# A 31-tap convolution on VectorE, its second channel tile's taps dealt out between the blocks of an attention

## The chip, the cores and the metric

The kernel runs on one core of a Trainium2 chip. The metric is the device time of one execution in microseconds (us). Of the runs of a kernel the median is given.

## What is computed

Two layers, each of a mixer and a feed-forward part, on 512 positions of 1024 features in float32. The mixer splits one projection into four branches and projects their concatenation back:

```python
za, zq, zkv, zg, zc, zd = jnp.split(rms_norm(x, g) @ w_in[l], offsets, axis=-1)
y_conv = conformer_conv(za, ...)      # gate, 31-tap causal depthwise conv, layer_norm, silu
y_nsa  = nsa_attention(q, kv, ...)    # compressed + selected + window attention, 4 heads of 64
y_sgu  = spatial_gating(zc, ...)      # gelu, layer_norm of v, 128x128 causal mix, times u
y_pool = multiscale_pool(zd, ...)     # running means over 2, 4, 8, 16
x = x + rms_norm(jnp.concatenate([y_conv, y_nsa, y_sgu, y_pool], -1) @ w_out[l], g2)
x = x + rms_norm(conv_ffn(rms_norm(x, g3), ...), g4)
```

Attention works on four blocks of 128 queries. With 512 positions all key blocks are selected, so block `i` has scores of width 128 (i + 1) in each of two branches (selected, window), and a third branch over 31 compressed keys.

## The kernel before

Activations lie with features on partitions, 128 to a tile. A product in float32 precision is three matmuls of a split into high and low parts (`product`, lines 149, 152 and 153); `split` makes the two parts of an activation, `yh`/`yl`, on ScalarE and VectorE or GpSimd.

`mixer` runs named steps in the order of the table `STEPS`. Their instructions are then put into one queue for each engine by a scheduler that models the times of the engines; each engine works its queue in order. So the table, data and buffers set the order together. `behind` adds an order between two instructions without a wait of its own.

The steps that matter here, by name:
- `taps`: 26 of the 31 taps of the depthwise convolution, for two channel tiles `j`, on VectorE (line 681, the first tap line 679), each adding to a PSUM accumulator `acc[j]` of pool tag `c`. Tile 1 runs `AHEAD = 12` taps behind tile 0, and the two alternate. `others` makes the last five taps on ScalarE and GpSimd, `sum` adds them.
- `cn` (`conv_norm`): the layer norm of the convolution and its Silu. A matmul with ones gives the mean (line 709), VectorE subtracts it, ScalarE squares, a second matmul with ones gives the variance (line 239 in `stats`), ScalarE takes the root, VectorE the reciprocal (line 242), GpSimd multiplies, ScalarE makes the Silu (line 722) and `split` the tiles y[0] and y[1].
- `a0` to `a3` and `b0` to `b3` (`scores`): for a block and a branch, four heads' scores on TensorE (lines 782 to 786), the maxima on VectorE (line 788), the exponentials on ScalarE (line 790), then the scaling of the probabilities (line 796).
- `p0` to `p3` (`values`): transposes of the probabilities (line 807), their copies out of PSUM (lines 811 on VectorE, 813 on ScalarE), the products with the values (line 816), at the end the compressed branch's (line 819), into y[2] and y[3].
- `cmp2` and `probs`: the compressed branch; its probabilities are multiplied on GpSimd and transposed by TensorE (line 752).
- `v`, `w`, `su`, `fg`: spatial gating, with the normalisation of v on VectorE; `fg` (line 658) makes y[4] and y[5].
- `pool0`, `pool1`, `fp`: pooling; `fp` (line 608) makes y[6] and y[7].

Behind the mixer comes `out_proj`, with y in the order 4, 5, 6, 7, 0, 1, 2, 3. Products whose y is there already can be placed by the scheduler among the last attention blocks.

PSUM has eight banks, handed out by pool tag: `s` 2, `t` 1, `o` 1, `mm` 2, `c` 2. Scores use `s`, and for blocks 2 and 3 `c` as a third bank; transposes `t`, and for blocks 2 and 3 also `c`.

Of the kernel before, what the change touches and what calls it, by code (L numbers as in the profile page):

```python
# [10 lines left out]
OP = mybir.AluOpType  # L11
AX = mybir.AxisListType

L, D, S = 2, 1024, 512
# [4 lines left out]
TAPS = 31  # L19
# [37 lines left out]
class Kernel:  # L57
# [6 lines left out]
    P_DVE, PT_DVE = ((2, 3), (2,), (0, 1), ()), (1, 0, 0)  # L64

    SQ_POOL = (1,), (1, 2, 3, 4, 5, 6, 7)

    AHEAD = 12

    LAST_POOL = (1, 4)  # L70

# [318 lines left out]
    def first_weights(self, l):  # L390
        return [self.weights(l, u) for u in (U_KK, U_CMP, U_Q, U_Q + 1)]

    STEPS = ("conv0", "consts", "conv1", "cmp", "kk", "q1", "nat", "w", "q0", "gates", "a1", "cmp2", "taps", "probs", "su",
             "v", "pool0", "a0", "b0", "b1", "p0", "p1", "pool1", "a2", "b2", "p2", "a3", "fp", "b3", "p3", "fg",
             "others", "sum", "cn")

    def mixer(self, l):
        nc = self.nc
# [5 lines left out]
        n = 512 if l == 0 else 256  # L404
# [4 lines left out]
        gl = [self.slot(f"z{j}", F, (128, 544)) for j in range(2)]  # L409
        acc = [None, None]  # L410
# [3 lines left out]
        def proj(u, tag="mm"):  # L414
            ps = self.ps(tag)
            m["proj"] = self.product(ps, self.weights(l, u), range(KT), h)
            return ps
# [88 lines left out]
        def probs():  # L506
# [4 lines left out]
        steps = {  # L511
            "consts": constants, "nat": nat, "gates": gates, "kk": keys, "cmp": lambda: m.update(g1=self.compressed(l, psc)),
            "cmp2": lambda: self.compressed_out(m["g1"]), "probs": probs,
            "su": lambda: self.gating_u([proj(U_SU + j) for j in range(2)]),
            "v": lambda: self.gating_v(m["nat"]), "w": self.gating_w, "fg": lambda: self.gating_finish(m["nat"]),
            "taps": lambda: self.taps(gl, acc), "others": lambda: self.other_taps(gl),
            "sum": lambda: self.taps_sum(acc), "fp": self.pool_finish, "cn": lambda: self.conv_norm(acc)}
# [4 lines left out]
        for i in range(4):  # L522
# [2 lines left out]
                    {(i, b): self.scores(i, b, m["gates"], Q2, KH, KL)})  # L525
            steps[f"p{i}"] = lambda i=i: self.values(i, [m[i, b] for b in range(2)], m["nat"], m["pcT"])
        for name in self.STEPS:
            steps[name]()

    def compressed(self, l, ps):  # L530

# [136 lines left out]
    def taps(self, gl, acc):  # L668

        nc = self.nc  # L670
        acc[:] = [self.ps("c") for _ in range(2)]
        n = TAPS - self.OTHER_TAPS
        for i in range(n + self.AHEAD):
            for j, k in ((0, i), (1, i - self.AHEAD)):
                if not 0 <= k < n:
                    continue
                x, w = gl[j][:, k:k + S], self.col("taps", j * TAPS + k)
                if k == 0:
                    nc.vector.tensor_scalar(acc[j], x, w, self.col("conv_b", j), op0=OP.mult, op1=OP.add)
                else:  # L680
                    nc.vector.scalar_tensor_tensor(acc[j], x, w, acc[j], op0=OP.mult, op1=OP.add)  # L681

    def other_taps(self, gl):
        nc = self.nc
# [73 lines left out]
    def scores(self, i, b, gates, Q2, KH, KL):  # L758

        nc = self.nc
        w = (i + 1) * 128
        e = max(w, 256)
        per = 1 if i > 1 else 2
        if i == 0:
            p = self.slot(("yh6", "yl6")[b])
            P = [p[:, 128 * s:128 * s + 128] for s in range(4)]  # L770
        elif i == 1:
            p = [self.slot("yh7"), self.slot("yl7")] if b == 0 else [self.tmp(), self.tmp()]
            P = [p[s // 2][:, 256 * (s % 2):256 * (s % 2) + 256] for s in range(4)]
        else:
            P = [self.slot(f"hl{4 * b + s}")[:, :w] for s in range(4)]
        sm = self.mp.tile([128, 3, 4], F, name="sm", tag="sm", bufs=3)
        for s0 in range(0, 4, per):
            ps = self.ps(("s", "s", "c")[self.sc % 3] if i > 1 else "s")
            self.sc += 1
            for s in range(s0, s0 + per):  # L780
                q, o = Q2[ORDER[s]][:, i * 128:(i + 1) * 128], 256 * (s - s0)
                nc.tensor.matmul(ps[:, o:o + e], q, KH[b][:, :e], start=s == s0, stop=False, skip_group_check=True)
                self.scored = nc.tensor.matmul(ps[:, o:o + e], q, KL[b][:, :e], start=False, stop=False,
                                               skip_group_check=True)
            src = ps.rearrange("p (s k) -> p s k", s=per)[:, :, :w]
            nc.tensor.matmul(src[:, :, w - 128:], self.identb, self.maskb[:, None, :].to_broadcast([128, per, 128]),
                             start=False, stop=True, skip_group_check=True)
            nc.vector.tensor_reduce(sm[:, 0, s0:s0 + per], src, axis=AX.X, op=OP.max, negate=True)
            for s in range(s0, s0 + per):
                nc.scalar.activation(P[s], src[:, s - s0], AF.Exp, bias=sm[:, 0, s:s + 1],  # L790
                                     accum_out=sm[:, 1, s:s + 1])
        nc.vector.reciprocal(sm[:, 2], sm[:, 1])
        self.tt(sm[:, 2], sm[:, 2], gates[:, 1 + b, 4 * i:4 * i + 4], OP.mult)
        for s in range(4):
            eng = nc.vector if s in self.P_DVE[i] else nc.gpsimd
            eng.tensor_scalar(P[s], P[s], sm[:, 2, s:s + 1], 0.0, op0=OP.mult, op1=OP.add)
        return P

    def values(self, i, P2, nat, pcT):

        nc = self.nc
        O = self.ps("o")
        for b, P in enumerate(P2):
            for kb in range(i + 1):
                pst = self.ps(("t", "c")[self.pt % 2] if i > 1 else "t")
                for s in range(4):
                    nc.tensor.transpose(pst[:, s * 128:(s + 1) * 128], P[s][:, kb * 128:(kb + 1) * 128], self.ident)
                PT = self.tmp() if i < 2 else self.slot(f"hh{self.pt % 8}")
                self.pt += 1
                if self.PT_DVE[self.pt % len(self.PT_DVE)]:  # L810
                    nc.vector.tensor_copy(PT, pst)
                else:
                    nc.scalar.activation(PT, pst, AF.Copy)
                v = nat[:, kb, 256 + 64 * b:320 + 64 * b]
                for c in range(2):
                    nc.tensor.matmul(O[64 * c:64 * c + 64, :256], v, PT[:, 256 * c:256 * c + 256],  # L816
                                     start=b == 0 and kb == 0, stop=False, skip_group_check=True)
        for t in range(2):
            nc.tensor.matmul(O[:, t * 128:(t + 1) * 128], self.vcbd[:, t * 128:(t + 1) * 128],
                             pcT[:, i * 128:(i + 1) * 128], start=False, stop=t == 1, skip_group_check=True)  # L820
        for t in range(2):
            c = slice(i * 128, (i + 1) * 128)
            hi, lo = self.y[2 + t]
            nc.scalar.activation(hi[:, c], O[:, t * 128:(t + 1) * 128], AF.Copy)
            self.tt(lo[:, c], O[:, t * 128:(t + 1) * 128], hi[:, c].bitcast(F), OP.subtract)
# [117 lines left out]
def layouts(i):  # L943
# [30 lines left out]
    for n, ph in enumerate(PHASES):  # L974
        for j in range(8):
# [10 lines left out]
    out["vec"] = np.concatenate(  # L986
        [part(i[n]) for n in ("norm_mix_pre", "norm_mix_post", "norm_ffn_pre", "norm_ffn_post", "conv_dw_b",
                              "conv_ln_g", "conv_ln_b", "pool_scale", "sgu_ln_g", "sgu_ln_b")] + [pe, taps, fw, fb], axis=2)
    out["sgu_b"] = i["sgu_b"]
    out["wst"] = i["sgu_w"].transpose(0, 3, 1, 2)  # L990
# [52 lines left out]
```

## Time and profile before

| | |
|---|---|
| three runs | 1198.51, 1198.56, 1205.59 us; median 1198.56 |
| the profiled execution | 1195.33 us, span 1193.5 us |
| TensorE busy | 1132.3 us, 95% |
| VectorE busy | 746.2 us, 63% |
| ScalarE busy | 597.6 us, 50% |
| GpSimd busy | 553.9 us, 46% |

The span is the stretch that the trace covers; the execution's own time is 1.8 us longer. The shares are averages over the whole span. The mixers take up about 40 to 175 us (layer 0) and 640 to 765 us (layer 1); the rest is output projection, norms and feed-forward.

### The profile page before, as it was taken

What the parts mean: (1) busy time and instruction counts of PE and PEld (TensorE: products, weight loads), DVE (VectorE), ACT (ScalarE), POOL (GpSimd) and SP (SyncE); (2) the same over time, 40 slices, a digit from 0 to 9 for tenths busy, and PEclk for the clock granted to TensorE, in tenths of its full rate; (3) what the DMA queues carried; (4) which work ended last, traced back from release to release, by engine and by line L of the source; (5) the groups of instructions that cost most, each with busy time, mean ns of one, the idle gap of its engine ahead of it and who ended that gap; (6) DMA issues with size and microseconds to landing.
All of it is one profiled execution on the core that took longest, in us unless ns stands there. A gap on an engine that the chain in (4) does not pass through costs nothing.

```text
span 1193.5 us, 15945 instructions
## 1 busy us (share of the span) xinstructions
PE 1132.3 (95%) x6070; PEld 938.4 (79%) x6070; DVE 746.2 (63%) x1076; ACT 597.6 (50%) x973; POOL 553.9 (46%) x480
## 2 busy tenths in 40 slices
PE   7998999898999999999989979999999999999995
PEld 6786579886888888888978856899868888888894
DVE  5799734786076614774568997247942665157736
ACT  7777656554334323333657956564543443233431
POOL 1354443365655555554244544424656555455532
PEclk9999899999999999999999989999999999999997
DMA  8869015423432323223638660162233332322302
GB/s 266 225 161 215 12 49 145 103 85 93 141 90 96 97 96 99 89 89 88 165 63 212 148 158 1 35 166 64 95 102 124 93 102 71 123 89 89 90 35 71
DMA packets 43213, 129.35 MB, mean 108 GB/s; under 512 B 6144, under 2 KB 9856, under 8 KB 43136
## 3 DMA queue, kind: packets, MB, share of 16 engines
q1 hardware_dynamic: 35648, 102.01, 27.1%
q0 software_dynamic: 7488, 26.32, 11.9%
q8 instruction: 48, 0.79, 0.3%
q14 instruction: 29, 0.24, 0.1%
HBM read 126.21 MB, written 2.10 MB: 108 GB/s over the span
## 4 chain that ended last, share of the span: by engine, by line
PE 64%; DVE 19%; DMA 7%; ACT 6%; issue 3%; SPq 1%; POOL 0%; DVEq 0%; ACTq 0%
PE ps_s L153 7%; PE ps_s L149 7%; PE ps_s L152 7%; PE ps_mm L149 7%; PE ps_mm L153 7%; PE ps_mm L152 6%; PE ps_c L149 6%; PE ps_c L152 6%; PE ps_c L153 6%; DMA raw<-in_ws_dram 5%; DVE ps_c L681 4%; DVE q L888 2%; PE ps_o L816 2%; DVE yl L101 2%; DVE q L101 1%
## 5 line engine op out<-in xcount | busy, mean ns | idle before, releaser
L101 POOL TENSOR_TENSOR wlo<-raw,whi 128x512 fp32r<-128x512 f32 (+1 forms) x252 | 358.1, 1445 | 304.5 <-ACT whi L126 290.3
L126 ACT ACTIVATE whi<-raw 128x1024 fp32r<-128x1024 f32 (+2 forms) x180 | 183.7, 1024 | 156.8 <-DMA raw<-in_ws_dram 59.1
L149 PE MATMUL ps_mm<-hh,whi 128*128 128x512 f32 (+1 forms) x368 | 141.4, 384 | 9.6 <-ACT nat L447 3.9
L153 PE MATMUL ps_mm<-hh,wlo 128*128 128x512 f32 (+1 forms) x368 | 140.4, 382 | 1.8 <-DMA wlo<-in_ws_dram 1.7
L888 DVE SCALAR_TENSOR_TENSOR q<-q,vec,q 128x511 f32<-128x511 f32 (+1 forms) x88 | 115.4, 1317 | 40.4 <-ACT q L885 39.1
L152 PE MATMUL ps_mm<-hl,whi 128*128 128x512 f32 (+1 forms) x368 | 139.8, 380 | 0.0
L135 POOL DMA_DIRECT2D wlo<-in_ws_dram x52 | 45.9, 886 | 171.8 <-ACT wlo L134 118.5
L149 PE MATMUL ps_s<-hh,whi 128*128 128x512 f32 (+1 forms) x312 | 115.7, 373 | 8.5 <-ACT whi L362 7.1
L152 PE MATMUL ps_s<-hl,whi 128*128 128x512 f32 (+1 forms) x312 | 116.4, 373 | 1.2 <-DVE hl L278 1.1
L153 PE MATMUL ps_s<-hh,wlo 128*128 128x512 f32 (+1 forms) x312 | 115.1, 369 | 2.2 <-DMA wlo<-in_ws_dram 2.2
L153 PE MATMUL ps_c<-hh,wlo 128*128 128x512 f32 (+1 forms) x288 | 107.1, 372 | 1.5 <-DMA wlo<-in_ws_dram 1.5
L149 PE MATMUL ps_c<-hh,whi 128*128 128x512 f32 (+1 forms) x288 | 107.4, 373 | 0.8 <-ACT hh L273 0.8
L152 PE MATMUL ps_c<-hl,whi 128*128 128x512 f32 (+1 forms) x288 | 107.0, 372 | 0.0
L149 PEld LDWEIGHTS ps_mm<-hh,whi 128*128 128x128 f32 x368 | 70.5, 191 | 24.8 <-ACT nat L447 4.1
L153 PEld LDWEIGHTS ps_mm<-hh,wlo 128*128 128x128 f32 x368 | 70.4, 191 | 16.6 <-DMA wlo<-in_ws_dram 2.3
L149 PE MATMUL ps_mm<-yh,whi 128*128 128x256 f32 (+1 forms) x236 | 79.4, 336 | 2.8 <-ACT yh L158 2.7
L152 PEld LDWEIGHTS ps_mm<-hl,whi 128*128 128x128 f32 x368 | 70.6, 192 | 13.8
L152 PE MATMUL ps_mm<-yl,whi 128*128 128x256 f32 (+1 forms) x236 | 78.5, 333 | 0.2 <-DVE yl L101 0.2
L153 PE MATMUL ps_mm<-yh,wlo 128*128 128x256 f32 (+1 forms) x236 | 78.6, 333 | 0.0
L888 DVE SCALAR_TENSOR_TENSOR kl<-kl,vec,kl 128x511 f32<-128x511 f32 (+1 forms) x44 | 58.8, 1336 | 25.9 <-ACT kl L885 25.2
L149 PEld LDWEIGHTS ps_s<-hh,whi 128*128 128x128 f32 x312 | 59.1, 189 | 20.0 <-ACT whi L362 7.1
L152 PE MATMUL ps_s<-yl,whi 128*128 128x512 f32 (+1 forms) x222 | 73.6, 332 | 0.0
(331 smaller groups left out, 2670.7 us busy)
## 6 DMA issues: line engine op xcount, KB each, us to landing
raw<-in_ws_dram SPq DMA_DIRECT2D x156, 512.0 KB, 3.6
wlo<-in_ws_dram POOLq DMA_DIRECT2D x44, 512.0 KB, 7.3
raw<-in_ws_dram SPq DMA_DIRECT2D x16, 384.0 KB, 3.1
tmp<-in_w_dram SPq DMA_DIRECT2D x16, 256.0 KB, 5.3
raw<-in_ws_dram SPq DMA_DIRECT2D x8, 396.0 KB, 4.1
wlo<-in_ws_dram POOLq DMA_DIRECT2D x8, 396.0 KB, 7.4
x<-in_xt_dram SPq DMA_DIRECT2D x8, 256.0 KB, 5.4
out_dram<-x SPq DMA_DIRECT2D x16, 128.0 KB, 1.8
```

What stands on the lines that cost most here:

```text
L101: return (eng or self.nc.vector).tensor_tensor(out, x, y, op=op)
L126: one = nc.scalar.activation(hi[:, :cols], raw[:, :cols], AF.Copy)
L135: nc.gpsimd.dma_start(lo[:, :cols], src, accum_op=OP.add)
L149: one = nc.tensor.matmul(ps, wh, ah, start=start and n == 0, stop=False)
L152: nc.tensor.matmul(ps, wh, al, start=False, stop=False)
L153: one = nc.tensor.matmul(ps, wl, ah, start=False, stop=stop and n == len(ks) - 1)
L681: nc.vector.scalar_tensor_tensor(acc[j], x, w, acc[j], op0=OP.mult, op1=OP.add)
L816: nc.tensor.matmul(O[64 * c:64 * c + 64, :256], v, PT[:, 256 * c:256 * c + 256], start=b == 0 and kb == 0, stop=False, skip_group_check=True)
L888: nc.vector.scalar_tensor_tensor(t[:, s:], v[:, :S - s], fw(k), t[:, s:], op0=OP.mult, op1=OP.add)
```

## The change

The taps of tile 0 now run alone, ahead of `a1`. Tile 1's 26 taps are cut into groups (`"t0:5"` is taps 0 to 4), and each tap of a group is put behind the maxima that were written last, `self.topped`. The compressed branch (`cmp2`, `probs`), `su` and `a0` now come ahead of `v` and the pooling steps, `p0` ahead of `pool1`, `fg` ahead of `b2` and `fp` behind `p2`. The third bank of blocks 2 and 3 comes from tag `mm` in place of `c`, for scores and for transposes. No operation is added or left out.

```diff
-    AHEAD = 12
...
-    STEPS = ("conv0", "consts", "conv1", "cmp", "kk", "q1", "nat", "w", "q0", "gates", "a1", "cmp2", "taps", "probs", "su",
-             "v", "pool0", "a0", "b0", "b1", "p0", "p1", "pool1", "a2", "b2", "p2", "a3", "fp", "b3", "p3", "fg",
-             "others", "sum", "cn")
+    STEPS = ("conv0", "consts", "conv1", "cmp", "kk", "q1", "nat", "w", "q0", "gates", "taps", "a1", "t0:0",
+             "cmp2", "probs", "su", "a0", "t0:5", "v", "b0", "t5:10", "b1", "t10:14", "pool0", "p0", "pool1",
+             "p1", "a2", "t14:18", "fg", "b2", "t18:22", "p2", "fp", "a3", "t22:26", "b3", "p3", "others",
+             "sum", "cn")
...
         for name in self.STEPS:
-            steps[name]()
+            if ":" in name:
+
+                self.some_taps(gl, acc, 1, range(*map(int, name[1:].split(":"))), self.topped)
+            else:
+                steps[name]()
...
         acc[:] = [self.ps("c") for _ in range(2)]
-        n = TAPS - self.OTHER_TAPS
-        for i in range(n + self.AHEAD):
-            for j, k in ((0, i), (1, i - self.AHEAD)):
...
+        self.some_taps(gl, acc, 0, range(TAPS - self.OTHER_TAPS))
+
+    def some_taps(self, gl, acc, j, ks, behind=None):
+        nc = self.nc
+        for k in ks:
+            x, w = gl[j][:, k:k + S], self.col("taps", j * TAPS + k)
+            if k == 0:
+                one = nc.vector.tensor_scalar(acc[j], x, w, self.col("conv_b", j), op0=OP.mult, op1=OP.add)
+            else:
+                one = nc.vector.scalar_tensor_tensor(acc[j], x, w, acc[j], op0=OP.mult, op1=OP.add)
+            self.behind(one, behind)
...
-            ps = self.ps(("s", "s", "c")[self.sc % 3] if i > 1 else "s")
+            ps = self.ps(("s", "s", "mm")[self.sc % 3] if i > 1 else "s")
...
-            nc.vector.tensor_reduce(sm[:, 0, s0:s0 + per], src, axis=AX.X, op=OP.max, negate=True)
+            self.topped = nc.vector.tensor_reduce(sm[:, 0, s0:s0 + per], src, axis=AX.X, op=OP.max, negate=True)
...
-                pst = self.ps(("t", "c")[self.pt % 2] if i > 1 else "t")
+                pst = self.ps(("t", "mm")[self.pt % 2] if i > 1 else "t")
```

Line numbers of the changed kernel differ by -2 to +4: maxima stand in line 792, taps in 684 (the first of a tile in 682), transposes in 811, the values' products in 820 and 823, the ones matmuls of `conv_norm` in 713 and 237.

VectorE's queue in layer 1 before, around block 0's maxima of the second branch (line 788, the first such row here; `z_5427` and `z_5428` are the padded inputs of the convolution's tiles 0 and 1, `z_6664` the sum of tile 0, the `cmx` rows the compressed branch):

```order
L681 SCALAR_TENSOR_TENSOR ps_c<-z_5427,vec,ps_c 128x512
L101 TENSOR_TENSOR sm<-sm,gates 128x4
L101 TENSOR_TENSOR z_6291<-ps_mm,rsx 128x512
L101 TENSOR_TENSOR z_6099<-yh_6102,z_6099 64x16
L788 TENSOR_REDUCE sm<-ps_s 128x2 x2
L681 SCALAR_TENSOR_TENSOR ps_c<-z_5428,vec,ps_c 128x512
L101 TENSOR_TENSOR cmx<-cmx,gates 128x16
L101 TENSOR_TENSOR z_6099<-yl_6104,z_6099 64x16
L101 TENSOR_TENSOR z_6664<-ps_c,yh_6636 128x512
```

The same engine in the changed kernel, from the sum of tile 0 to the first taps of tile 1; the maxima here are those of block 0's first branch:

```order
L99 TENSOR_TENSOR z_6664<-ps_c,yh_6636 128x512
L636 TENSOR_SCALAR nat<-nat,bmv,bsd 128x256 x4
L99 TENSOR_TENSOR z_6018<-ps_mm,rsx 128x512
L745 TENSOR_REDUCE cmx<-ps_o 128x16
L792 TENSOR_REDUCE sm<-ps_s 128x2 x2
L682 TENSOR_SCALAR ps_c<-z_5428,vec 128x512
L99 TENSOR_TENSOR tmp<-ps_o,cmx 128x512
L684 SCALAR_TENSOR_TENSOR ps_c<-z_5428,vec,ps_c 128x512
L796 RECIPROCAL sm<-sm 128x4
```

Before, tile 0 is finished and tile 1 nearly so when block 0's second maxima are taken; now tile 0 is finished ahead of the first, and tile 1 begins behind them.

TensorE's queue in layer 1 before, at the variance matmul of `conv_norm` (line 239; `hl` are probabilities of block 3, `yh_6616` a tile of y[4] to y[7] in a product of the output projection, `whi` and `wlo` its weights):

```order
L807 MATMUL ps_t<-ident,hl_6491 128x128
L807 MATMUL ps_c<-ident,hl_6491 128x128 x2
L239 MATMUL ps_mm<-tmp,ones 128x512
L807 MATMUL ps_t<-ident,hl_6492 128x128
L807 MATMUL ps_c<-ident,hl_6492 128x128 x2
L149 MATMUL ps_mm<-yh_6616,whi 128x256
L152 MATMUL ps_mm<-yl_6617,whi 128x256
L153 MATMUL ps_mm<-yh_6616,wlo 128x256
```

The same engine in the changed kernel, at the variance matmul (line 237):

```order
L811 MATMUL ps_t<-ident,hl_6525 128x128
L820 MATMUL ps_o<-hh_6617,nat 64x256 x2
L820 MATMUL ps_o<-hh_6626,nat 64x256 x2
L823 MATMUL ps_o<-pct,vcbd 128x128 x2
L237 MATMUL ps_mm<-tmp,ones 128x512
L147 MATMUL ps_mm<-yh_6347,whi 128x256
L150 MATMUL ps_mm<-yl_6348,whi 128x256
L151 MATMUL ps_mm<-yh_6347,wlo 128x256
```

The variance matmul has moved from among block 3's transposes to behind the last matmul of p3 (line 823). Behind it stand 24 matmuls of 256 columns, then the first product with a normalised tile, `yh_6684`; in layer 0 12 of 512 and 12 of 256 columns.

## Rows read from the trace of the kernel before

**Rows 1.** The page: busy times; the chain by engine; loads on SP's queue.

```profile
PE 1132.3 (95%) x6070; PEld 938.4 (79%) x6070; DVE 746.2 (63%) x1076; ACT 597.6 (50%) x973; POOL 553.9 (46%) x480
...
PE 64%; DVE 19%; DMA 7%; ACT 6%; issue 3%; SPq 1%; POOL 0%; DVEq 0%; ACTq 0%
...
raw<-in_ws_dram SPq DMA_DIRECT2D x156, 512.0 KB, 3.6
```

**Rows 2.** Windows: length, busy time of PE, PEld, DVE, ACT, POOL; then granted clock.

```profile
110.00:120.00 10.00, 5.82 (x32) 4.42 (x31) 7.99 (x21) 4.80 (x15) 7.34 (x8) 0.81 0.92 201
120.00:130.00 10.00, 8.84 (x44) 5.61 (x42) 8.77 (x24) 6.78 (x23) 5.90 (x9) 0.68 0.04 7
690.00:700.00 10.00, 8.95 (x45) 6.86 (x44) 10.00 (x19) 7.03 (x14) 3.19 (x4) 1.00 1.06 261
700.00:710.00 10.00, 3.56 (x14) 2.88 (x15) 9.84 (x25) 3.11 (x15) 6.75 (x8) 0.67 0.49 112
710.00:720.00 10.00, 9.26 (x53) 6.32 (x53) 9.73 (x27) 6.60 (x21) 4.32 (x8) 0.82 0.01 2
```

**Rows 3.** The same view of the two stretches at the lower clock.

```profile
116.00:126.00 10.00, 8.06 (x30) 5.28 (x31) 7.25 (x22) 6.02 (x24) 6.27 (x9) 0.51 0.38 72
703.30:713.20 9.90, 6.76 (x26) 5.16 (x27) 9.80 (x26) 5.03 (x20) 7.39 (x9) 0.50 0.28 55
```

**Rows 4.** TensorE's waits over the span: total, times, longest.

```profile
PE ps_s L782 <- ACT yl L790: 6.6, 2, 5.8
...
PE ps_t L752 <- POOL tmp L101: 2.7, 1, 2.7
```

**Rows 5.** The chain that ended last, in layer 1: start, length, what.

```profile
665.58 8.10 DVE ps_c L681 x13
...
703.88 0.67 DVE sm L788 x2
```

**Rows 6.** Timeline of VectorE at the end of layer 1's mixer.

```profile
752.90 3.35 DVE L242 RECIPROCAL tmp<-tmp 128x512 f32<-128x512 f32 x1 [7.46 <-ACT tmp L240]
756.17 0.63 DVE L811 COPY hh<-ps_c 128x512 f32<-128x512 f32 x1
```

**Rows 7.** The chain at the end of both mixers, layer 0 first.

```profile
160.66 0.86 PE ps_mm L239 x2
...
172.06 0.64 PE ps_o L819 x4
172.82 0.24 PE ps_mm L149
...
749.95 0.86 PE ps_mm L239 x2
...
761.15 0.64 PE ps_o L819 x4
```

**Rows 8.** Timeline of ScalarE at the end of layer 1's mixer.

```profile
750.89 1.28 ACT L240 ACT_TABLE_LOAD   x1 [6.17 <-PE ps_mm L239]
752.18 0.69 ACT L240 ACTIVATE tmp<-ps_mm,eps 128x512 f32<-128x512 f32 x1
...
756.49 1.28 ACT L722 ACT_TABLE_LOAD   x1
...
758.63 0.63 ACT L158 ACTIVATE yh<-z 128x512 fp32r<-128x512 f32 x1
```

**Rows 9.** Timeline of TensorE: starts of successive matmuls of 512 columns.

```profile
757.22 0.40 PE L152 MATMUL ps_c<-yl,whi 128*128 128x512 f32 x1
757.46 0.39 PE L153 MATMUL ps_c<-yh,wlo 128*128 128x512 f32 x1
```

**Rows 10.** Windows with other idle time of TensorE; the wait in the first.

```profile
620.00:630.00 10.00, 6.92 (x26) 5.27 (x26) 1.75 (x1) 9.83 (x15) 1.76 (x2) 0.91 0.61 105
630.00:640.00 10.00, 10.00 (x41) 7.98 (x40) 9.77 (x17) 6.84 (x9) 4.04 (x4) 0.92 0.83 195
...
PE ps_mm L149 <- ACT rsx L240: 3.1, 1, 3.1
```

More of the change, by code (lines that the diff above doesn't have):

```diff
@@ L671, in taps @@
         acc[:] = [self.ps("c") for _ in range(2)]
-        n = TAPS - self.OTHER_TAPS
-        for i in range(n + self.AHEAD):
-            for j, k in ((0, i), (1, i - self.AHEAD)):
[L675 to L681, printed above, removed]
+        self.some_taps(gl, acc, 0, range(TAPS - self.OTHER_TAPS))
[8 more added lines that the diff above has]
+            self.behind(one, behind)
     def other_taps(self, gl):
```

## The prediction

> **What bounds the kernel now.** I began with the page. TensorE is busy 95% of the span and carries 64% of the chain that ended last, VectorE 19% [rows 1]. So the kernel is a matmul kernel, and time can be won only where TensorE stands still or runs at its lower clock. Next I read the table of windows over the two mixers, to find such places. In layer 0 TensorE is busy 5.82 of the 10 us from 110 and 8.84 of the next ten; in layer 1 8.95, 3.56 and 9.26 of the thirty from 690 [rows 2]. Idle, that is 5.3 and 8.2 us. VectorE is full there (9.84 of 10 in the worst window). After the idle time the granted clock is 0.50, the 1.2 GHz level, for about ten microseconds per layer, in which TensorE is busy 8.06 and 6.76 us [rows 3]; at 2.4 GHz that work would have taken half, so 4.0 and 3.4 us more went there. **The prize is 5.3 + 4.0 = 9.3 us in layer 0 and 8.2 + 3.4 = 11.6 us in layer 1**, 20.9 us in all.
>
> The list of TensorE's waits says who ends the idle time: the exponentials of block 0's second branch (5.8 us at one time), and the product that the compressed branch leaves on GpSimd (2.7 us) [rows 4]. Both descend from VectorE. The chain of layer 1 shows why VectorE is late: 8.10 us of it are 13 convolution taps in a row, and block 0's second maxima come only at 703.88 [rows 5].
>
> **What the change takes out of the front.** Nothing is added or dropped: the same 26 + 26 taps run in each layer. Counted in the order, 24 taps of tile 1 stand ahead of block 0's second maxima in layer 0 and 21 in layer 1 now; in the changed kernel there are 5. That is 19 and 16 taps fewer; by the spacing in the run of thirteen (8.10 / 13 = 0.62 us, [rows 5]) 11.8 and 9.9 us of VectorE. This is an upper end for what those maxima can come earlier, not the gain. They also need ScalarE, whose queue has weight conversions between the exponentials, and earlier scores on TensorE. Following the rows of layer 0 through the new order, with the durations of the trace, I get a VectorE that waits some 3 us for ScalarE ahead of block 0's second exponentials, pooling's operations that now stand between b0's and b1's maxima, and b1's scores about 4.7 us earlier. In layer 1, where the wait of 5.8 us is one piece and fewer other operations are between, the exponentials of block 0 come about 6 us earlier, and the wait that they ended goes, with most of the half clock.
>
> The taken-out taps come back later: five groups, 4 or 5 taps each, between the maxima of b0 to a3. There VectorE has room now (in layer 0 it is idle 3.2 us of the 20 from 110, [rows 2]), but it works in order, and the copies of the transposed probabilities (0.63 us, [rows 6]) and the next maxima stand behind taps. One copy in block 1 has seven taps ahead of it, 4.3 us; TensorE cannot transpose into that bank until the copy is done. The scores and transposes get their third bank from the pool of the gating and pooling products now instead of the convolution's; I cost that at nothing, since those products come behind a2 and p2, and at one copy, 0.6 us, if two users meet. Moving pooling behind b1 hides it behind TensorE's scores as before. The gating weights for layer 1 come by a DMA that VectorE's product now meets earlier; the stall lies between 0 and the 3.6 us in which a load of the same queue lands [rows 1]. I take 0, since VectorE reaches that product only behind block 2's first maxima, and keep 3.6 in the upper end.
>
> I take a **lead at the end of attention of 3.8 us in layer 0** (4.7 less one such copy's wait) **and 7 us in layer 1** (between the 6 that I followed and the prize of 11.6). The ends I keep are 2 and 9.3, and 3 and 11.6.
>
> **What the change does at the back.** This is where I chose against the gain. With tile 1's last taps behind a3 and b3, the convolution's normalisation starts later, and the order shows TensorE's matmul for its variance (L239 before) directly behind the last matmul of p3. In the trace of before it lies eleven microseconds ahead of that end (160.66 against 172.06 in layer 0, 749.95 against 761.15 in layer 1), and the first product with the normalised tile starts right at the end of p3, at 172.82 [rows 7]: the chain is hidden under output-projection products that wait for nothing.
>
> Its length is to be read in layer 1, from the matmul at 749.95: a table load and a square root on ScalarE from 750.89, the reciprocal on VectorE (3.35 us), GpSimd's product, another table load, Silu, and the rounding that ends at 758.63 + 0.63 = 759.26 [rows 6, 8]. **9.3 us**, each step waiting for the one before it. In the changed kernel only few matmuls stand between that variance matmul and the first that needs its result: in layer 0 12 of 512 columns and 12 of 256, in layer 1 24 of 256. Two matmuls of 512 columns follow each other after 0.24 us [rows 9]; I take 0.235, and half of it, 0.118, for 256, so 12 x 0.235 + 12 x 0.118 = 4.2 us and 24 x 0.118 = 2.8 us; with the variance matmul itself (0.86 us) 5.1 and 3.7 us of work. TensorE is left idle for 9.3 - 5.1 = **4.2 us in layer 0** and 9.3 - 3.7 = **5.6 us in layer 1**. Everything else of the output projection stands behind it in the queue, the attention's own tiles too.
>
> The products that filled this before ran ahead of p3's end and now run behind it, so they cancel. What is left is the idle time minus the lead: 4.2 - 3.8 = +0.4 us in layer 0, 5.6 - 7 = -1.4 us in layer 1. **-1.0 us** together.
>
> **The clock behind these new gaps.** The wait of 5.8 us in layer 1 was followed by the 0.50 stretch of [rows 3]. A wait of 3.1 us at the start of layer 1 left 0.91 and 0.92 in two windows of ten, 1.7 us of clock [rows 10]. The new gaps lie between the two: I take 2.4 us for 4.2, and 3.7 us for 5.6 (a stretch like that of layer 1, but over a queue that is full, would cost up to 4.1). The sum is -1.0 + 2.4 + 3.7 = **+5.1 us**. The profiled execution took 1195.33 us, so 1200.4; the median of the runs is 3.2 us above that execution, so on the scale of the runs **1203.6 us**.
>
> The Trainium skill, "TensorE: Matmul & The Clock Gate", section "Why this matters for your kernels", tells authors to leave no idle gaps between bursts of matmuls, since the clock then falls to its lower level; the 0.50 stretches agree. Taken strictly it speaks against this change, with a whole stretch behind both new gaps: 8.2 in place of 6.1 us, 1205.7.
>
> In the chain's rows the square root starts 1.29 us after the start of its table load, which takes 1.28. The Trainium skill, "ScalarE: Activation LUTs", section "What ACT_TABLE_LOAD costs", adds a drain of 1380 ns to each load. No such time is in the trace; by the page the two loads of each chain would make both gaps 2.8 us longer and the time about 1209, an estimate that the rows don't bear out.
>
> **The rivals.** (a) *The back stays hidden and the front is won.* If the normalisation ended under other matmuls after all, the whole prize could come: 1198.6 - 20.9 = 1177.7. The idle time and VectorE's taps ahead of it speak for that; the place of the variance matmul speaks against it, since its engine works in order. Full leads with the back's gaps but no half clock would give 4.2 - 9.3 + 5.6 - 11.6 = -11.1, 1187.5. (b) *The gaps at the back come, the clock stays.* -1.0 us: 1197.6, no change. For it: the gap of layer 0 is nearer to the 3.1 us wait than to the 5.8. (c) *Slower: VectorE, not the scores, becomes what attention waits for.* Each group of taps that stands ahead of a copy or of the next maxima stops TensorE for 2 to 4 us. With leads of only 2 and 3 us and a whole half-clock stretch behind each back gap: 4.2 - 2 + 5.6 - 3 + 8.2 = +13.0, 1211.6. It decides from the point at which tile 1's last tap ends too late for p3: between that tap and the variance matmul lie the mean's matmul and some six operations of 0.6 to 0.7 us on VectorE and ScalarE, about 5 us by estimate, and p3 of layer 0 would end at 172.7 - 5.1 - 3.8 = 163.8; so from about 159 us on each microsecond is one more of idle time. For it: VectorE is the fuller engine throughout this stretch; against it: the idle time that it has from 110 on now.
>
> **How the numbers follow.** My forecast, the back's gaps with a partly lowered clock, gets 0.43; (b) 0.25; (c) 0.19; (a) with its half-way cases 0.13. A measurement here can tell about 1% (12 us) from no change. Faster by more than that is (a): 0.13. Slower by more is the upper half of (c) and the tail of the forecast: 0.17. The rest, 0.70, is within. The range must reach from the better end of the forecast and (b), just short of full leads, 1189, to just above (c), 1214; the whole gain of (a) and a worse (c) are left out.
>
> **What would show it.** In the changed profile, TensorE's waits on block 0's exponentials and on the transposed compressed probabilities should be gone or under 2 us, and the clock near 1.00 at 116 to 126 and 703 to 713. In place of them I expect two waits on the rounded convolution tile (ScalarE, in the output projection's first products with it), of 4 and 6 us, at 165 to 175 and 755 to 765, and a half-clock stretch behind at least the second. TensorE's waits on copies of transposes should grow in blocks 1 and 2. If those back waits are absent, the step on the variance matmul is wrong and (a) holds; if the front waits are still there, the taps were not what held them.

## The result, and the profile after

The changed kernel takes 1217.49 us, the median of 4 runs (1215.63 to 1221.90), against 1199.55 us. The ratio is 1.0154, with a 95% interval of 1.0126 to 1.0182: slower by 18 us. The forecast was 1203.6, level, and the time lies above its range.

The profiled execution is the slowest of the four, with a span of 1220.1 us. A wait of 4.4 us for a weight transfer at 611 us, in the feed-forward part, stands in this execution (the list of waits below); whether the other three have it is not known. It lies outside the two stretches compared below, so the mixers' loss does not hang on it. Page of the changed kernel, busy times and the chain by engine:

```profile
PE 1139.8 (93%) x6070; PEld 945.6 (77%) x6070; DVE 745.5 (61%) x1076; ACT 598.2 (49%) x973; POOL 552.9 (45%) x480
...
PE 65%; DVE 16%; ACT 7%; DMA 7%; issue 3%; POOL 1%; SPq 1%; DVEq 0%; ACTq 0%
```

Against [rows 1], TensorE's busy time has grown by 7.5 us with the same 6070 matmuls, and VectorE's is the same. To place the loss I cut both traces at the same two matmuls of each layer, a norm's ones matmul ahead of the mixer and the first one behind the output projection. Windows of the kernel before, then of the changed one (length, busy time of PE, PEld, DVE, ACT, POOL, then granted clock):

```profile
24.88:193.38 168.50, 158.04 (x947) 125.44 (x946) 118.52 (x217) 113.47 (x210) 68.64 (x69) 0.96 0.54 131
618.92:782.95 164.03, 150.54 (x922) 120.38 (x921) 117.00 (x215) 112.91 (x210) 67.89 (x69) 0.96 0.44 104
```

```profile
25.98:204.68 178.70, 159.79 (x947) 126.72 (x946) 117.40 (x217) 113.73 (x210) 67.62 (x69) 0.96 0.50 123
636.06:809.13 173.07, 152.15 (x921) 121.82 (x920) 117.76 (x215) 113.59 (x210) 67.73 (x69) 0.96 0.43 98
```

Layer 0 is 10.2 us longer, layer 1 9.0 us. TensorE's idle time (length less busy) goes from 10.5 to 18.9 and from 13.5 to 20.9 us; the other 1.8 and 1.6 us are busy time. The lower clock does not explain that by itself: over each of the four windows the granted clock is 0.96, so the clock that was won at the front was lost again elsewhere. Together the layers are 19.2 us longer, about the 18 us of the medians; the two profiled executions lie 26.6 us apart, and the rest is outside these windows. The same view by tens of microseconds, to be held against [rows 2]:

```profile
80.00:90.00 10.00, 6.74 (x37) 5.34 (x36) 9.56 (x22) 9.91 (x17) 1.75 (x2) 0.88 0.82 194
90.00:100.00 10.00, 10.00 (x44) 7.82 (x42) 3.82 (x13) 9.84 (x14) 3.24 (x5) 0.95 0.65 180
...
110.00:120.00 10.00, 9.59 (x68) 7.85 (x66) 9.49 (x24) 5.26 (x14) 6.94 (x9) 1.00 0.59 126
120.00:130.00 10.00, 7.59 (x54) 4.86 (x54) 9.68 (x23) 6.23 (x22) 5.57 (x7) 1.00 0.53 124
130.00:140.00 10.00, 7.35 (x37) 4.17 (x38) 9.93 (x20) 2.38 (x7) 1.79 (x3) 0.83 0.00 0
...
180.00:190.00 10.00, 7.79 (x34) 6.63 (x35) 0.00 (x0) 4.83 (x7) 4.27 (x4) 0.83 0.00 0
...
720.00:730.00 10.00, 6.46 (x44) 5.16 (x46) 8.17 (x20) 3.85 (x14) 5.08 (x7) 0.66 0.56 121
...
780.00:790.00 10.00, 4.98 (x23) 4.26 (x24) 3.35 (x1) 5.98 (x8) 5.07 (x4) 0.86 0.00 0
790.00:800.00 10.00, 10.00 (x67) 9.21 (x66) 1.54 (x3) 5.98 (x14) 4.49 (x4) 0.97 0.20 54
```

The hole at 110 to 126 is smaller and its long stretch at 0.50 is gone, but the idle time has moved to 120 to 140, where VectorE is now full (9.93), and to the end of the mixer. At 80 to 100, where the granted clock was 1.00 before, it is 0.88 and 0.95. TensorE's waits over the span, against [rows 4] (total, times, longest):

```profile
PE ps_mm L147 <- ACT yh L156: 7.0, 3, 4.2
PE ps_c L151 <- DMA wlo<-in_ws_dram: 4.7, 2, 4.4
PE ps_s L147 <- ACT yh L156: 4.6, 1, 4.6
PE ps_mm L661 <- DVE z L99: 4.0, 1, 4.0
...
PE ps_mm L147 <- DVE bs L649: 3.3, 1, 3.3
PE ps_o L820 <- ACT hh L817: 3.3, 5, 0.9
```

The two waits on block 0's exponentials and on GpSimd's product are gone. In their place stand the rounded convolution tile (4.2 and 4.6 us, ends of the two mixers), gating's finish (line 661), which waits for a bank of pool `mm` until VectorE has read pooling's product out of it, and the weights' bias of gating (line 649). The last row is waits on copies of the transposes; at the same place (line 816) the kernel before has 0.7 us. The bias is a price of the taps: in layer 0 VectorE makes it behind the last fifteen taps of tile 0 and the tile's sum (timeline of VectorE).

```profile
73.56 11.83 DVE L684 SCALAR_TENSOR_TENSOR ps_c<-z,vec,ps_c 128x512 f32<-128x512 f32 x15
...
86.11 0.60 DVE L649 SCALAR_TENSOR_TENSOR bs<-ps_mm,vec,bs 128x128 f32<-128x128 f32 x2
```

Every run below with tile 0's taps first has this wait (2.6 to 5.7 us), and none with the two tiles alternating. The end of layer 0 in the chain, against [rows 7] and [rows 8] (start, length, what):

```profile
172.15 0.66 PE ps_o L823 x4
172.83 0.29 ACT yh L828
173.14 0.30 DVE yl L99
173.47 0.24 ACT yh L828
173.76 1.28 ACT L238
175.06 0.70 ACT tmp L238
175.78 3.36 DVE tmp L240
179.22 1.27 POOL z L99
180.51 0.82 ACT z L726
181.36 0.64 ACT yh L156
182.06 1.29 POOL yl L99
183.40 0.79 PE ps_mm L150
```

For ten microseconds the chain is off TensorE, from p3's last matmul to the first products with the normalised tile. In [rows 7] it went on at once.

### The profile page after: what moved, and what is told of

Same layout as the page of the kernel before. It is cut to its first block, busy times and chain, and to the rows that moved or that the text cites. A ratio compares the mean times of both kernels' runs of the same rounds, so it can differ in the third digit from the quotient of the medians.

```text
span 1220.1 us, 15934 instructions
## 1 busy us (share of the span) xinstructions
PE 1139.8 (93%) x6070; PEld 945.6 (77%) x6070; DVE 745.5 (61%) x1076; ACT 598.2 (49%) x973; POOL 552.9 (45%) x480
## 3 DMA queue, kind: packets, MB, share of 16 engines
q0 software_dynamic: 7488, 26.32, 11.9%
## 4 chain that ended last, share of the span: by engine, by line
PE 65%; DVE 16%; ACT 7%; DMA 7%; issue 3%; POOL 1%; SPq 1%; DVEq 0%; ACTq 0%
PE ps_mm L151 7%; PE ps_mm L150 7%; PE ps_mm L147 7%; PE ps_s L150 7%; PE ps_s L151 7%; PE ps_s L147 7%; PE ps_c L151 6%; PE ps_c L150 6%; PE ps_c L147 6%; DMA raw<-in_ws_dram 4%; DVE ps_c L684 3%; DVE q L892 2%; DMA wlo<-in_ws_dram 2%; DVE yl L99 1%; ACT wlo L132 1%
## 5 line engine op out<-in xcount | busy, mean ns | idle before, releaser
L147 PE MATMUL ps_s<-yh,whi 128*128 128x256 f32 (+1 forms) x222 | 73.7, 332 | 4.6 <-ACT yh L156 4.6
L684 DVE SCALAR_TENSOR_TENSOR ps_c<-z,vec,ps_c 128x512 f32<-128x512 f32 x100 | 74.8, 748 | 1.5
```

The costliest lines, as they stand in the source:

```text
L147: one = nc.tensor.matmul(ps, wh, ah, start=start and n == 0, stop=False)
L684: one = nc.vector.scalar_tensor_tensor(acc[j], x, w, acc[j], op0=OP.mult, op1=OP.add)
```

## The experiments

Theory A, from the prediction: the normalisation has gone behind p3, because tile 1's taps end late, and its waits are the loss. Rival B: the groups of taps and the new order lose the time in front and middle. The first four runs were made on these.

**Without the normalisation.**

```diff
-        s = self.tmp()
-        self.tt(s, acc[0], acc[1], OP.add)
...
-            self.tt(acc[j], acc[j], rs, OP.mult, self.eng("cn"))
```

> The changed kernel without the normalisation of the convolution: mean, variance, root and reciprocal are left out, Silu works on the plain sum. Theory A (the chain that now stands behind p3 is the main loss): both waits on the rounded convolution tile (4.2 and 4.6 us) and the half clock behind them go, with two ones matmuls of 0.86 us per layer: 1217.5 - 8.8 - 3.4 - 3.4 = about 1202. Rival B (the loss is made ahead of p3's end, by tap groups and the new order, and the end only shows it): the chain's waits go but other waits come at the same place, 1211 to 1217.

1218.94 us, ratio 1.0161 (1.0130 to 1.0192). The waits at the back are gone, and the time is not. But the scheduler made another order for this program, and its trace has two long waits far ahead of the part that was taken out, the first of them 3.3 us in the changed kernel and the second not there (timeline of TensorE, wait in brackets):

```profile
86.07 0.77 PE L147 MATMUL ps_mm<-hh,whi 128*128 128x512 f32 x1 [5.70 <-DVE bs L649]
115.16 0.58 PE L772 MATMUL ps_s<-kh,q 128*128 128x256 f32 x1 [5.51 <-ACT yh L780]
```

So it is no clean price of the chain, and no support for theory A either.

**New order, old taps and banks.**

```diff
-        self.some_taps(gl, acc, 0, range(TAPS - self.OTHER_TAPS))
+        n = TAPS - self.OTHER_TAPS
+        for i in range(n + self.AHEAD):
+            for j, k in ((0, i), (1, i - self.AHEAD)):
...
-            ps = self.ps(("s", "s", "mm")[self.sc % 3] if i > 1 else "s")
+            ps = self.ps(("s", "s", "c")[self.sc % 3] if i > 1 else "s")
...
-                pst = self.ps(("t", "mm")[self.pt % 2] if i > 1 else "t")
+                pst = self.ps(("t", "c")[self.pt % 2] if i > 1 else "t")
```

> The new order of steps with the taps of the kernel before (both tiles alternating, twelve apart, third bank again from the convolution's pool). If the splitting of tile 1's taps is the cause (A and the part of B on taps), 1195 to 1203; if the order of the other steps is, 1210 or more.

The groups are out of the table as well. 1200.42 us, ratio 1.0000 (0.9977 to 1.0022). The order of the other steps is not the loss by itself. In this trace the two waits of [rows 4] are gone too, with the taps alternating as before, so dealing the taps out was not needed to end them; and the time is level without them. This run undid two things at once, though, taps and banks.

**The normalisation earlier in the table.**

```diff
-             "p1", "a2", "t14:18", "fg", "b2", "t18:22", "p2", "fp", "a3", "t22:26", "b3", "p3", "others",
-             "sum", "cn")
+             "p1", "a2", "t14:18", "fg", "b2", "t18:26", "others", "sum", "p2", "fp", "a3", "cn", "b3", "p3")
```

> The changed kernel with tile 1's last eight taps in one group behind b2, the sum there, and the normalisation ahead of b3. Theory A: the variance matmul is back among block 3's transposes, the 9 us of waits and 3.4 us of half clock at the back go: about 1205. Rival B: VectorE only gets fuller in block 2, TensorE waits there for copies what it gains at the back: 1212 to 1218.

1214.18 us, 1.0119 (1.0094 to 1.0144): 3 to 4 us won, not 12, and the interval overlaps that of the changed kernel.

**Old order, groups of taps and new banks.**

```diff
-    STEPS = ("conv0", "consts", "conv1", "cmp", "kk", "q1", "nat", "w", "q0", "gates", "taps", "a1", "t0:0",
-             "cmp2", "probs", "su", "a0", "t0:5", "v", "b0", "t5:10", "b1", "t10:14", "pool0", "p0", "pool1",
-             "p1", "a2", "t14:18", "fg", "b2", "t18:22", "p2", "fp", "a3", "t22:26", "b3", "p3", "others",
-             "sum", "cn")
+    STEPS = ("conv0", "consts", "conv1", "cmp", "kk", "q1", "nat", "w", "q0", "gates", "a1", "cmp2", "taps", "t0:0",
+             "probs", "su", "v", "pool0", "a0", "t0:5", "b0", "t5:10", "b1", "t10:14", "p0", "p1", "pool1", "a2",
+             "t14:18", "b2", "t18:22", "p2", "a3", "t22:26", "fp", "b3", "p3", "fg", "others", "sum", "cn")
```

> The order of steps of the kernel before, with tile 1's taps in the same groups behind the same maxima and the third bank from the products' pool; only the order of the other steps is undone. If the order of the other steps is the cause, 1197 to 1203; if the groups of taps and the late normalisation are, 1213 to 1220.

1219.21 us, 1.0159 (1.0136 to 1.0183). The whole loss is in the taps or in the banks.

Reading the orders of these four gave theory C. In the run with the old taps the variance matmul stands right behind p2; in the order of the next run, with the new banks, it stands behind p3 although the taps are early. `conv_norm` takes its banks from `mm`, and now so do the transposes, which the table puts ahead of it until p3 ends. So the bank change, which I had priced at nothing, would be the cause.

**The banks alone, on the new order with old taps.**

```diff
-            ps = self.ps(("s", "s", "c")[self.sc % 3] if i > 1 else "s")
+            ps = self.ps(("s", "s", "mm")[self.sc % 3] if i > 1 else "s")
...
-                pst = self.ps(("t", "c")[self.pt % 2] if i > 1 else "t")
+                pst = self.ps(("t", "mm")[self.pt % 2] if i > 1 else "t")
```

> As the run with the new order and the old taps, which took 1200.4, with one thing added: the third bank of blocks 2 and 3, for scores and transposes, from the pool of the products (mm) as in the changed kernel. In the order the variance matmul then stands behind p3's last matmul, although the taps are as early as before. Theory C (the bank change, not the late taps, puts the normalisation behind p3, since conv_norm takes its banks from the same pool): two waits of 4 to 6 us on the rounded convolution tile with half clock behind, 1209 to 1214. If the groups of taps are the whole cause: 1198 to 1203.

1215.60 us, 1.0153 (1.0132 to 1.0173): from 1.0000 to the changed kernel's ratio by these two lines. The waits at the back are those of the changed kernel, with taps that end early (timeline of TensorE):

```profile
177.88 0.50 PE L149 MATMUL ps_mm<-yh,whi 128*128 128x512 f32 x1 [4.25 <-ACT yh L158]
...
781.23 0.79 PE L149 MATMUL ps_s<-yh,whi 128*128 128x512 f32 x1 [4.57 <-ACT yh L158]
```

**The normalisation's matmuls from pool `c`.** The same edit on the changed kernel and on the run just told:

```diff
-        ps = self.ps("mm")
+        ps = self.ps("c")
         nc.tensor.matmul(ps, self.ones, s, start=True, stop=True)
...
-        self.stats("mm", sq[0], S, 1.0 / 256, self.eps[:, 1:2], rs)
+        self.stats("c", sq[0], S, 1.0 / 256, self.eps[:, 1:2], rs)
```

> The changed kernel with one thing changed: the two ones matmuls of the convolution's normalisation take their banks from the convolution's pool (c). In the order the variance matmul is back ahead of p3's end. Theories A and C: the waits at the back (8.8 us) and the half clock behind them (3.4 us) go, 1205 to 1208. Rival B (the loss is made in the front and middle): 1213 to 1219.

1212.81 us, 1.0117 (1.0086 to 1.0148). The waits at the back are gone, 4.7 us are won where 10 to 12 were expected, and the interval overlaps that of the changed kernel.

> New order, old taps, third bank from the products' pool, and the normalisation's matmuls from the convolution's pool. Theory C: the place of the variance matmul is what the bank change costs, so 1197 to 1203. If sharing the products' pool costs in the middle as well: 1205 to 1210.

1207.37 us, 1.0080 (1.0065 to 1.0095). Of the bank change's 1.5% the place of the normalisation is about half (1.0153 to 1.0080); the rest is made ahead of it. Part of that is gating's finish, which waits for its `mm` bank here (1.4 us in layer 0, 2.8 in layer 1) and doesn't in the run with the old banks. In the trace of the changed kernel with this edit that wait is even longer than before the edit (timelines of TensorE of the two runs):

```profile
711.16 1.98 PE L662 MATMUL ps_mm<-wst,nat 128*64 128x128 f32 x16 [2.81 <-DVE z L101]
...
718.46 1.97 PE L661 MATMUL ps_mm<-wst,nat 128*64 128x128 f32 x16 [5.74 <-DVE z L99]
```

**One group, normalisation from `c`.** Tile 1's taps in one group (`"t0:26"` behind `a1`).

```diff
-             "cmp2", "probs", "su", "a0", "t0:5", "v", "b0", "t5:10", "b1", "t10:14", "pool0", "p0", "pool1",
-             "p1", "a2", "t14:18", "fg", "b2", "t18:22", "p2", "fp", "a3", "t22:26", "b3", "p3", "others",
+             "t0:26", "cmp2", "probs", "su", "a0", "v", "b0", "b1", "pool0", "p0", "pool1",
+             "p1", "a2", "fg", "b2", "p2", "fp", "a3", "b3", "p3", "others",
```

> The changed kernel with tile 1's 26 taps in one group behind a1's maxima, tile 0 ahead of them, and the normalisation's matmuls from the convolution's pool. Against the run with both tiles alternating and the same banks it shows what finishing tile 0 first costs: 1197 to 1204 if nothing. Rival B, tile 0's chain in one piece delays what stands behind it: 1206 or more.

1206.14 us, 1.0074 (1.0050 to 1.0097), level with the alternating tiles: with these banks finishing tile 0 first costs nothing that can be measured.

**The bank change alone undone, in the changed kernel.**

```diff
-            ps = self.ps(("s", "s", "mm")[self.sc % 3] if i > 1 else "s")
+            ps = self.ps(("s", "s", "c")[self.sc % 3] if i > 1 else "s")
...
-                pst = self.ps(("t", "mm")[self.pt % 2] if i > 1 else "t")
+                pst = self.ps(("t", "c")[self.pt % 2] if i > 1 else "t")
```

> The changed kernel, groups of taps and order of steps as they are, with the bank change alone undone: the third bank of scores and transposes comes from the convolution's pool (c) again, of which tile 1's accumulator holds one bank for long. Theory C (the bank change is the loss): 1195 to 1203, level with the kernel before or a little under it. If the groups of taps cost by themselves, or the one bank that is left in that pool is too few: 1206 or more.

1205.30 us, 1.0048 (1.0028 to 1.0068): some 12 of the 18 us come back. 0.5% is left, just above what theory C alone allows. The taps end as late as in the changed kernel, and the variance matmul stands ten microseconds ahead of p3's end again (layer 0 below), without a wait at the back. So late taps don't put it there. Gating's finish still waits (timeline of TensorE):

```profile
165.02 1.02 PE L237 MATMUL ps_mm<-tmp,ones 128*128 128x512 f32 x2
...
175.14 0.71 PE L823 MATMUL ps_o<-pct,vcbd 128*128 128x128 f32 x4
...
712.86 1.98 PE L661 MATMUL ps_mm<-wst,nat 128*64 128x128 f32 x16 [4.21 <-DVE z L99]
```

**Which of the two users of `mm`.** A third bank for scores alone (transposes only `"t"`), and a second bank for transposes alone (scores only `"s"`):

```diff
-                pst = self.ps(("t", "mm")[self.pt % 2] if i > 1 else "t")
+                pst = self.ps("t")
```

> The changed kernel with a third bank (mm) for scores alone; transposes have one bank. The order has the variance matmul ahead of p3's end. Theory C says that the transposes, which come until the end of p3, keep the products' pool from the normalisation: no waits of 4 us at the back; the transposes' second bank is missing, so 1203 to 1212.

1218.41 us, 1.0157 (1.0123 to 1.0191). The back is free, as the order said, but the expectation of the time was wrong. A single bank for transposes would then cost about as much; no run has it by itself, so this is not shown.

```diff
-            ps = self.ps(("s", "s", "mm")[self.sc % 3] if i > 1 else "s")
+            ps = self.ps("s")
```

> The changed kernel with the second bank (mm) for transposes alone; scores have two banks. The order has the variance matmul behind p3's last matmul. Theory C: the 4 us waits at the back are there, 1213 to 1221.

1219.76 us, 1.0166 (1.0142 to 1.0189), with waits of 4.3 and 4.6 us at the back. It is the transposes that hold the normalisation up. Neither half of the bank change is a way out.

**One group, banks from `c`.** The edit of the one group (`"taps", "a1", "t0:26"`), with the banks undone:

```diff
-            ps = self.ps(("s", "s", "mm")[self.sc % 3] if i > 1 else "s")
+            ps = self.ps(("s", "s", "c")[self.sc % 3] if i > 1 else "s")
...
-                pst = self.ps(("t", "mm")[self.pt % 2] if i > 1 else "t")
+                pst = self.ps(("t", "c")[self.pt % 2] if i > 1 else "t")
```

> New order, tile 0's taps first, tile 1's 26 in one group behind a1's maxima, third bank from the convolution's pool. Theory C: 1195 to 1201; if tile 0 first and tile 1 later is by itself a loss: 1204 or more.

1203.24 us, 1.0034 (1.0016 to 1.0052): a little slower than the kernel before, as with the groups. Against the same order with both tiles alternating (1.0000) the intervals just touch.

**The kernel before with the bank change alone.**

```diff
-            ps = self.ps(("s", "s", "c")[self.sc % 3] if i > 1 else "s")
+            ps = self.ps(("s", "s", "mm")[self.sc % 3] if i > 1 else "s")
...
-                pst = self.ps(("t", "c")[self.pt % 2] if i > 1 else "t")
+                pst = self.ps(("t", "mm")[self.pt % 2] if i > 1 else "t")
```

> The kernel before with the bank change alone: the third bank of blocks 2 and 3 from the products' pool. Taps and order of steps are as before. Theory C: the gating products and the normalisation, both from that pool, come behind p3: 1213 to 1222. If the bank change only hurts together with the new order: 1197 to 1204.

1218.03 us, 1.0168 (1.0132 to 1.0204). Old taps, old order, and two words make the whole loss. TensorE's waits (total, times, longest):

```profile
PE ps_mm L149 <- ACT yh L158: 5.7, 3, 2.9
...
PE ps_mm L782 <- DVE z L101: 4.4, 2, 2.7
...
PE ps_s L149 <- ACT yh L158: 4.1, 1, 4.1
...
PE ps_mm L709 <- DVE tmp L101: 2.2, 2, 1.2
```

Block 2's scores wait for pooling's products to leave their bank (line 782), and mean and normalised tile are late at the back.

**The same with the normalisation from `c`.**

```diff
-        ps = self.ps("mm")
+        ps = self.ps("c")
         nc.tensor.matmul(ps, self.ones, s, start=True, stop=True)
...
-        self.stats("mm", sq[0], S, 1.0 / 256, self.eps[:, 1:2], rs)
+        self.stats("c", sq[0], S, 1.0 / 256, self.eps[:, 1:2], rs)
```

> The same with the normalisation's matmuls from the convolution's pool. In the order gating's matmuls and the mean's are still behind p3, so other banks alone don't bring the normalisation forward here: 1211 to 1222 if its place counts and not its pool; 1200 to 1208 if the pool counts by itself.

1219.73 us, 1.0168 (1.0135 to 1.0201). Here the other pool doesn't bring the mean's matmul forward, in the order it stays behind p3, and nothing is won. Its place counts, not the pool as such; what holds it there in the old order no run shows.

**Banks undone and gating's finish behind p3, in the changed kernel.**

```diff
-             "p1", "a2", "t14:18", "fg", "b2", "t18:22", "p2", "fp", "a3", "t22:26", "b3", "p3", "others",
+             "p1", "a2", "t14:18", "b2", "t18:22", "p2", "fp", "a3", "t22:26", "b3", "p3", "fg", "others",
```

> The changed kernel with the bank change undone and gating's finish behind p3, as before; against the run with the bank change alone undone (1205.3, ratio 1.0048) it tells whether the rest of the loss is gating's early place: 1196 to 1201 then, with the groups of taps free. If the groups make the rest: 1204 to 1208.

1199.96 us, 1.0005 (0.9987 to 1.0023). With the groups of taps in and these two things undone the kernel is level with the one before. Windows between the same two matmuls of each layer:

```profile
24.94:192.93 167.99, 156.09 (x948) 124.94 (x946) 117.13 (x217) 114.39 (x210) 67.79 (x69) 0.96 0.54 132
621.42:784.91 163.49, 150.46 (x922) 119.47 (x921) 116.81 (x215) 113.51 (x210) 68.94 (x69) 0.96 0.46 104
```

In this one execution each layer is 0.5 us shorter than before. VectorE's taps are out of block 0's way, and the idle time of TensorE is 11.9 and 13.0 us, about what it was (10.5 and 13.5). The timeline of its TensorE shows where it went: in layer 0 it waits for gating's bias behind tile 0's taps, and in layer 1 the scores of block 2 now wait for block 1's exponentials.

```profile
85.72 0.77 PE L147 MATMUL ps_mm<-hh,whi 128*128 128x512 f32 x1 [5.20 <-DVE bs L649]
...
710.30 0.69 PE L786 MATMUL ps_s<-kh,q 128*128 128x384 f32 x1 [4.80 <-ACT tmp L794]
```

ScalarE was idle itself ahead of those exponentials, for 4.4 us, until VectorE had block 1's maxima. On VectorE the five taps 5 to 9 and pooling's operations stand ahead of these maxima (timelines of VectorE and ScalarE; the first row is the last of the five):

```profile
706.19 0.74 DVE L684 SCALAR_TENSOR_TENSOR ps_c<-z,vec,ps_c 128x512 f32<-128x512 f32 x1
...
708.43 0.68 DVE L792 TENSOR_REDUCE sm<-ps_s 128x2 f32<-128x512 f32 x1
...
709.23 0.47 ACT L794 ACTIVATE tmp<-ps_s,sm 128x256 f32<-128x256 f32 x1 [4.44 <-DVE sm L792]
```

So it is VectorE again that ends the idle time, with work that includes taps taken from ahead of block 0's maxima.

**Old taps and banks, new order, gating's finish behind p3.** On the run with the old taps:

```diff
-             "p1", "a2", "fg", "b2", "p2", "fp", "a3", "b3", "p3", "others",
+             "p1", "a2", "b2", "p2", "fp", "a3", "b3", "p3", "fg", "others",
```

> The new order with the old taps and banks (1200.4, ratio 1.000) and gating's finish behind p3: what is left of the change is the compressed branch, block 0 and p0 ahead of gating's v and pooling. If that earlier attention gains by itself: 1188 to 1195, faster than both kernels; if not: 1197 to 1203.

1208.34 us, 1.0086 (1.0054 to 1.0118). Slower, where the same kernel with gating's finish ahead of b2 is level. So that step's place helped with the groups of taps (1.0048 to 1.0005) and hurt without them (1.0000 to 1.0086). Why is left open; the place changes the schedule of everything behind block 1.

No version beat the kernel before.

## Why the prediction was wrong

**What bounds the kernel, and the prize: right as a reading.** The waits named in [rows 4] are gone in the changed trace, and layer 0's stretch at 0.50 with them; of layer 1's some 7 us are left (0.66 over ten microseconds, 720 to 730). But layer 0 has others: the granted clock is 0.88, 0.95 and 0.83 at 80 to 90, 90 to 100 and 130 to 140. And the run with the old taps lost the same two waits by the order of steps alone, and was level.

**The waits at the back: right in size, wrong in cause.** I worked out 4.2 and 5.6 us of idle time; the trace has 4.2 us, and in layer 1 4.6 us and 0.7 us ahead of it. The chain from variance matmul to rounded tile took 9.4 us (172.63 to 181.99) against 9.3. The half clock behind was over-sized: the window at 0.83 is 1.7 us of clock, those at 0.86 and 0.97 together 1.7 as well, against my 2.4 and 3.7. But I put the place of the normalisation down to late taps. The run with early taps and new banks has the same waits, and the one with late taps and old banks has none.

**The step that failed** is the sentence on the third bank, "I cost that at nothing, since those products come behind a2 and p2, and at one copy, 0.6 us, if two users meet". The two lines alone, in the kernel before, cost 1.0168, some 20 us. Different runs show what they did. They put the normalisation behind p3: with other banks for it the run with the old taps won 0.7%, the changed kernel about 0.4%, which is not clear of noise. In the kernel before they made block 2's scores wait for pooling's products (1.7 and 2.7 us), and on the new order with old taps gating's finish (1.4 and 2.8 us). The waits on copies at line 820 are 3.3 us there too, as in the changed kernel, against 0.7 with the old banks and 0.9 with the normalisation from `c`, so they come with the banks and not with the groups. The 4.0 us for which gating's finish waits in the changed kernel are not theirs alone: with the banks undone it waits 4.2 us. I looked for the price of the bank in the copies that use it, and it was paid by the steps that had lost it.

**The lead**, which I took as 3.8 and 7 us, was the term through which this came in. p3's last matmul in layer 0 stands at 172.08 against 171.99, with the layer's start 1.1 us later: 1.0 us ahead, but with 5.1 us of products less in front of it. That is a lead of -4.1 us. In layer 1 it is (761.08 - (776.68 - 17.14)) - 3.7 = -2.2 us, 17.14 being the later start. The two terms are off by 7.9 and 9.2 us. With the clock at 3.4 us where I had 6.1, and the idle time at 9.5 where I had 9.8, the forecast of +5.1 becomes the 19.2 us of the two windows. The 3.8 us were not worked out cleanly either: 4.7 less a copy's wait is 3.8 only for a wait of 0.9 us, and the prediction prices one at 0.6 or 4.3. The lead was there up to p0: its last matmul stands at 126.28 against 127.93. It was lost between p0 and p1, in waits on copies and exponentials, and through p3, which ran alone where it used to be filled.

**The rivals.** (c) had the nearest time, 1211.6, and the right sign. Its mechanism is in the traces, but it is the smaller part. In the changed kernel VectorE reads pooling's product, for which gating's finish waits, at 722.79, behind the same taps 5 to 9. On the new order with the old banks the groups cost 0.5% (1.0000 to 1.0048), with gating's finish behind p3 they win 0.8% (1.0086 to 1.0005), and with the new banks they change nothing (1.0153 and 1.0154). So the two losses don't add up, and (c) came near without the bank change in its sum, which is luck. (a) failed even with the old banks and gating's finish behind p3: the named waits were gone, and VectorE brought others, 5.2 us for gating's bias and 4.8 us by way of block 1's exponentials. The forecast has its piece of luck as well: the change with the bank change alone undone took 1205.30 us, close to 1203.6, but the waits at the back, on which the forecast was built, are not in its trace.

## What to carry to other kernels

A change that moves a buffer from one pool to another is priced at the steps that shared the new pool, and the lowest in the order pay first: here the normalisation, which no edit touched, fell behind everything that had been given its banks. Look up in the order where the last users of the pool now stand before asking how long the new users hold a bank. And work that is taken from ahead of one wait, but stays on its engine, stands ahead of another: here the taps behind block 0's maxima stood ahead of block 1's, so that VectorE ended the next idle time as well, although the list of waits names ScalarE. When a list of waits names an engine, look up what that engine was waiting for.

## What the runs showed of the hardware

The load of Silu's table doesn't wait for Silu's input: in layer 0 of the changed kernel it starts at 175.76, right behind the root, and Silu itself at 180.51 (timeline of ScalarE), so it is hidden behind reciprocal and product:

```profile
175.76 1.28 ACT L726 ACT_TABLE_LOAD   x1
180.51 0.81 ACT L726 ACTIVATE z<-z,vec 128x512 f32<-128x512 f32 x1 [3.47 <-POOL z L99]
```

I had counted that load as a link of the chain ([rows 8]), where it stood behind a copy and ended just ahead of Silu. It is not one. The chain's length was about the same without it, 9.4 us, since ScalarE took p3's output (172.83 to 173.76) ahead of the root.
